# w2's seven products: the sums R1, R6 and R7 over the chunks in DRAM, by adding transfers, instead of in SBUF by the vector engine

## The chip, the core and the metric

One core of one Trainium2 chip runs the whole program. The time is that of the device, in microseconds (us), from one launch; several runs give a median. Beside it there is one profiled execution, whose trace gives the start and the length of every instruction.

Five engines work at the same time, each through its own list of instructions in order: TensorE (PE in the profile; its weight loads are PEld), VectorE (DVE), ScalarE (ACT), GpSimd (POOL) and SyncE (SP). An instruction that waits holds up everything behind it on its engine. SP issues the loads of the weights; in the part that matters here POOL has little else to do than to issue transfers too.

## What is computed

One layer of a network over 384 tokens (128 of a context, 256 latent ones) with D_MODEL 2048, all in float32. The change lies in the second half of the MLP:

```python
h = _rmsnorm(x, norm_w[2]) * (1 + scale_f) + shift_f
y = jnp.square(jax.nn.relu(h @ w1)) @ w2          # w1: 2048 x 8192, w2: 8192 x 2048
x = x + gate_f * _rmsnorm(y, norm_w[3])
```

## The kernel before, in words

**Precision.** Each matrix product is made of three matmuls: both operands are split in a rounded part hi and a remainder lo, and hi·hi, hi·lo and lo·hi are summed in PSUM. So each tile of weights (128 x 1024) is loaded by SP into a raw buffer, copied to hi by ACT (L134, L1189), and subtracted into lo by DVE (L135, L1190) before PE can use it.

**The MLP.** The 8192 rows of w2 are worked through in eight chunks `ch` of 1024 (`for ch in range(8)`). In a chunk the kernel makes that part of the hidden layer (`w1_group`, four groups of 256 hidden channels) and multiplies it by the chunk's rows of w2, in four blocks `n` of 512 output columns. The groups of w1 for the next chunk stand between the blocks of w2. The result is summed over the chunks in SBUF, in `y[0]` (context tokens), `y[1]` and `y[2]` (the two halves of the latent tokens).

**The seven products.** Chunk 0 multiplies in the ordinary way (`mlp_out`). Chunks 1 to 6 use `mlp_seven` for all four blocks, chunk 7 for blocks 0 and 1: 26 blocks in all. There the latent tokens are multiplied by a fast scheme: tokens, rows of w2 and columns are each halved, and seven products of quarters, R1 to R7, take the place of eight. DVE makes the sums and differences of w2's quarters (L1225, L1231, L1235, L1239). The products stand in halves of PSUM banks of 512 columns: bank "16" holds R1 and R6, bank "23" R2 and R3, "45" R4 and R5, and the right half of "x7" holds R7 (its left half, and bank "yz", belong to the context tokens). R2 to R5 belong to one output quarter each, and `add` puts them into `y` at once. R1, R6 and R7 belong to several quarters, so they are summed over the chunks by themselves: `r16` (128 x 512 for each block `n`) and `r7` (128 x 256). In the first such chunk, 1, ACT copies the banks into them (L1246, L1247); in the 22 later blocks DVE adds the banks onto them (`add`, L1212).

**The end of the sums.** `seven_done(n)` (L1250 on) combines the finished sums into `y[1]` and `y[2]` by six DVE instructions (L1258 to L1264). For blocks 2 and 3 that is after chunk 6; for blocks 0 and 1 it stands in `done_late`, which chunk 7's last part calls step by step (`mlp_out` with `done`). Then `done` squares `y` on ACT (L1128) and multiplies it by the gate on DVE (L1133), `norm_y` makes the norm, and `residual` adds the input and stores the result (L1144, L1145).

**What sets the order.** The program's text is not the order of the instructions: a scheduler places each engine's list, apart from the last block of all (`last_part`, whose DVE instructions stand as written). SBUF tiles come from pools with a fixed number of buffers: four for hi and lo, three for one half of the raw tiles and two for the other, and 55 `slot` tiles. Chunk 7 begins with `load_tail`, which has POOL load the gate (`gf`) and the residual's input (`x1t`) into slots, each as a slot comes free. So POOL waits there for matmuls that read the slots last.

Of the kernel before, what the change touches and what calls it, by code (L numbers as in the profile page):

```python
# [7 lines left out]
F32 = mybir.dt.float32  # L8
F32R = mybir.dt.float32r
AF = mybir.ActivationFunctionType  # L10
ALU = mybir.AluOpType
AX = mybir.AxisListType

P = 128
# [29 lines left out]
def hymba_kernel(  # L44
# [6 lines left out]
    nc = tc.nc  # L51
# [8 lines left out]
    dram = ctx.enter_context(tc.tile_pool(name="dram", bufs=1, space=bass.MemoryType.DRAM))  # L60
# [401 lines left out]
    for s in range(NS):  # L462
        for ci, (kind, c0, w) in enumerate(chunks):
            k0, nk = ksteps[s]
            hi, lo, n = w_first if s == 0 and ci < 2 else load_chunk(s, ci, h_ins if s == 0 else ())
# [704 lines left out]
        for _ in side:  # L1170
            pass

    def mlp_seven(ch, n, strp, r16, r7, feeds=()):


        k0, c0, first = 8 * ch, 512 * n, ch == S_FIRST
# [16 lines left out]
        def product(m, half, row, tok, w, start=True, stop=True, js=range(4)):  # L1193

            acc = banks[m][:, 256 * half:256 * half + 256]
            for j in js:
                t = k0 + 2 * j
                xh, xl = hid["s", t + 1] if row == 2 else hid[t + row]
                xh, xl = xh[:, tok * P:(tok + 1) * P], xl[:, tok * P:(tok + 1) * P]
                if m == "x7" and half and ch > S_LAST:  # L1200
                    xh, xl = hid["d", t + 1]
                wh, wl = (v[:, 256 * j:256 * j + 256] for v in w)
                nc.tensor.matmul(acc, xh, wh, start=start and j == 0, stop=False)  # L1203
                nc.tensor.matmul(acc, xh, wl, start=False, stop=False)  # L1204
                nc.tensor.matmul(acc, xl, wh, start=False, stop=stop and j == 3)  # L1205
            if tok:
                for f in feeds:
                    f()

        def add(dst, m, half=None):  # L1210
            src = banks[m] if half is None else banks[m][:, 256 * half:256 * half + 256]
            nc.vector.tensor_tensor(dst, src, dst, op=ALU.add)  # L1212
# [29 lines left out]
        add(ys[0], "yz")  # L1242
        w = split(b21, "t4")
        product("45", 0, 1, 2, w)
        if first:
            nc.scalar.activation(r7[:, n], banks["x7"][:, 256:], AF.Copy)  # L1246
            nc.scalar.activation(r16[:, n], banks["16"], AF.Copy)  # L1247
        else:
            add(r7[:, n], "x7", 1)
            add(r16[:, n], "16")  # L1250
        add(ys[2], "45")

    def seven_done(n, r16, r7):

        tt = nc.vector.tensor_tensor
        ys = [y[i][:, 512 * n:512 * n + 512] for i in range(3)]
        r1, r6, v = r16[:, n, 0:256], r16[:, n, 256:], r7[:, n]
        tt(ys[1][:, 0:256], ys[1][:, 0:256], r1, op=ALU.add)  # L1258
        tt(r6, r6, r1, op=ALU.add)
        tt(v, v, r6, op=ALU.add)  # L1260
        tt(r6, r6, ys[2][:, 256:], op=ALU.add)
        tt(ys[1][:, 256:], ys[1][:, 256:], r6, op=ALU.add)
        y2 = ys[2].rearrange("p (a q) -> p a q", a=2)
        tt(y2, y2, v.unsqueeze(1).to_broadcast([P, 2, 256]), op=ALU.add)  # L1264
# [4 lines left out]
    for ch in range(8):  # L1269
        if ch < S_FIRST:  # L1270
            w1_group(4, (ff, fx), 386)
            mlp_out(ch, (ff, fx, fn))
            fn.finish()
            for g in range(5, 8):
                w1_group(g, (ff,))
        elif ch <= S_LAST:
            if ch == S_FIRST:
                fx.finish()
                while not vec.get("half"):
                    next(ff.gen)  # L1280
                for scope in (xb_scope, acc_scope, ada_scope):
                    scope.close()
                str_scope = ExitStack()
                strp = str_scope.enter_context(tc.tile_pool(name="strp", bufs=1, side="right", reuse_waits="tile"))
                vec.update(pool=strp, acc=strp, slab=512, bufs=3, half=False)
                ff.rate = RATE_GS
                r16, r7 = strp.tile([P, 4, 512], F32, name="r16"), strp.tile([P, 4, 256], F32, name="r7")
            for n in range(4):
                mlp_seven(ch, n, strp, r16, r7, (ff,))
                if n == 1:  # L1290
                    w1_group(4 * ch + 4, (ff,))
            if ch == S_LAST:
                ff.finish()
                for n in range(N_LAST, 4):
                    seven_done(n, r16, r7)
            for g in range(1, 4):
                w1_group(4 * ch + 4 + g, (ff,))
        else:
            load_tail()
            for n in range(N_LAST):  # L1300
                mlp_seven(ch, n, strp, r16, r7)

            def done_late():
                for n in range(N_LAST):
                    seven_done(n, r16, r7)
                    yield
                    for i in range(3):
                        done(i, 512 * n, 512 * n + 512)
                        yield

            fd = Feed(done_late(), 1.0)
            ws = mlp_out(ch, (fd,), done, N_LAST)
            fd.finish()
# [56 lines left out]
```

## Time and profile before

| | |
|---|---|
| median of 3 runs | 1690.77 us (1688.34 to 1690.98) |
| span of the profiled execution | 1686.4 us, 27861 instructions |
| PE busy | 1657.3 us (98%) |
| DVE busy | 1341.7 us (80%) |
| ACT busy | 752.3 us (45%) |
| POOL busy | 130.9 us (8%) |
| the last of the 26 blocks of seven products | ends on PE at about 1643.1 us of the span |

The profile gives the profiled execution's span, from its first to its last instruction, and no other time for it. The median run is 4.4 us longer than this span, the shortest run 1.9 us: what lies around the span (the start and the end of the program) is not in the trace.

How to read it: a row of the timeline gives the start, the length, the engine, the line, and how many instructions it stands for, and in brackets how long the engine sat idle before it and what ended that. The chain is followed back from the last instruction, at each step to what released it. Rows of a window give the time in which each engine was busy in that stretch. Matmuls are pipelined, and each is shown longer than its distance to the next.

### The profile page before, as it was taken

The page shows a single profiled execution, that of the slowest core. Times are in us where ns is not written, and L with a number is a line of the kernel's source. Part 1 is how long each engine was busy: PE and PEld are TensorE (multiplying, and loading weights), DVE is VectorE, ACT ScalarE, POOL GpSimd, SP SyncE. Part 2 cuts the span into 40 slices and gives each one's busy share as a digit, 9 for nine tenths or more (in the row PEclk, how much of TensorE's full clock was granted, in tenths as well). Part 3 has the DMA queues.
Part 4 walks back from the last instruction along what each step waited for, and adds up shares of the span by engine and source line. Part 5 has one row for each costly group of instructions (what it writes and reads, how often), then busy time and mean ns, then how long its engine had stood idle before and what let it go on. Part 6 is the DMA issues. An engine that isn't in the chain of part 4 may idle for free.

```text
span 1686.4 us, 27861 instructions
## 1 busy us (share of the span) xinstructions
PE 1657.3 (98%) x10965; PEld 1583.9 (94%) x10965; DVE 1341.7 (80%) x2009; ACT 752.3 (45%) x1225; POOL 130.9 (8%) x181
## 2 busy tenths in 40 slices
PE   6999999999999999999999999999999999999997
PEld 3888999999999989988999999999999999999996
DVE  3677769898998959997797688988588588588688
ACT  4432355555443345543444444444444444444443
POOL 0000002221000023530000000000000000000120
PEclk9999999999999999999999999999999999999999
DMA  9999858776789964754556245544344443443653
GB/s 305 324 297 304 276 153 256 245 248 221 236 265 308 312 206 126 218 153 137 157 169 195 87 138 178 155 150 142 109 150 127 124 139 113 149 125 111 185 184 134
DMA packets 258195, 320.95 MB, mean 190 GB/s; under 512 B 14752, under 2 KB 223248, under 8 KB 257680
## 3 DMA queue, kind: packets, MB, share of 16 engines
q1 hardware_dynamic: 250256, 303.41, 57.1%
q0 software_dynamic: 5856, 13.69, 2.8%
q10 hardware_dynamic: 1952, 2.07, 0.4%
q8 instruction: 86, 1.41, 0.3%
q14 instruction: 45, 0.37, 0.1%
HBM read 308.61 MB, written 10.51 MB: 189 GB/s over the span
## 4 chain that ended last, share of the span: by engine, by line
PE 83%; DVE 9%; DMA 3%; issue 2%; SPq 1%; ACT 1%; POOL 0%; DVEq 0%; ACTq 0%; POOLq 0%
PE acc_w L144 9%; PE acc_w L143 9%; PE acc_w L145 9%; PE v L476 4%; PE y L1204 4%; PE y L1203 4%; PE y L1205 4%; PE u L476 4%; PE acc_wo L143 3%; PE acc_wo L144 3%; PE acc_wo L145 3%; PE y_yz L1203 2%; PE y_yz L1205 2%; PE y_yz L1204 2%; DVE ada_acc L316 2%
## 5 line engine op out<-in xcount | busy, mean ns | idle before, releaser
L144 PE MATMUL acc_w<-h2l,hi_w 128*128 128x384 f32 (+1 forms) x1024 | 346.2, 338 | 0.5 <-DVE h2l L997 0.5
L143 PE MATMUL acc_w<-h2h,hi_w 128*128 128x384 f32 (+1 forms) x1024 | 344.2, 338 | 1.4 <-ACT h2h L993 1.2
L145 PE MATMUL acc_w<-h2h,lo_w 128*128 128x384 f32 (+1 forms) x1024 | 345.1, 337 | 0.0
L135 DVE TENSOR_TENSOR lo_w<-raw_w,hi_w 128x1024 fp32r<-128x1024 f32 x152 | 185.5, 1222 | 134.2 <-ACT hi_w L134 133.7
L134 ACT ACTIVATE hi_w<-raw_w 128x1024 fp32r<-128x1024 f32 x152 | 160.7, 1058 | 211.8 <-PE acc_w L144 95.2
L316 DVE SCALAR_TENSOR_TENSOR ada_acc<-ada_raw,sg,ada_acc 128x1024 f32<-128x1024 f32 (+1 forms) x240 | 252.1, 1082 | 1.9 <-DMA ada_raw<-in_ada_w_dram 1.9
L143 PEld LDWEIGHTS acc_w<-h2h,hi_w 128*128 128x128 f32 x1024 | 192.2, 188 | 3.1 <-ACT h2h L993 2.0
L144 PEld LDWEIGHTS acc_w<-h2l,hi_w 128*128 128x128 f32 x1024 | 192.5, 188 | 1.2 <-DVE h2l L997 0.8
L145 PEld LDWEIGHTS acc_w<-h2h,lo_w 128*128 128x128 f32 x1024 | 192.4, 188 | 0.3 <-DVE lo_w L135 0.2
L1189 ACT ACTIVATE hi_t<-w 128x1024 fp32r<-128x1024 f32 x104 | 109.6, 1060 | 118.6 <-DVE w L1225 33.6
L1190 DVE TENSOR_TENSOR lo_t<-w,hi_t 128x1024 fp32r<-128x1024 f32 x104 | 126.4, 1221 | 15.1 <-ACT hi_t L1189 14.7
L1190 DVE TENSOR_TENSOR lo_b<-w,hi_b 128x1024 fp32r<-128x1024 f32 x78 | 95.3, 1222 | 40.5 <-ACT hi_b L1189 40.4
L1189 ACT ACTIVATE hi_b<-w 128x1024 fp32r<-128x1024 f32 x78 | 82.6, 1060 | 99.2 <-PE acc_w L144 65.9
L134 ACT ACTIVATE hi_wo<-raw_wo 128x1024 fp32r<-128x1024 f32 x32 | 34.0, 1064 | 83.5 <-DMA raw_wo<-in_w_out_dram 65.7
L923 ACT ACTIVATE z<-acc_w 128x384 f32<-128x384 f32 x54 | 26.3, 487 | 75.0 <-PE acc_w L145 75.0
L476 PE MATMUL v<-hi_v,hh 128*128 128x384 f32 (+1 forms) x144 | 47.8, 332 | 0.0
L476 PE MATMUL v<-lo_v,hh 128*128 128x384 f32 (+1 forms) x144 | 46.6, 324 | 0.0
L476 PE MATMUL v<-hi_v,hl 128*128 128x384 f32 (+1 forms) x144 | 46.5, 323 | 0.0
L134 ACT ACTIVATE hi_v<-raw_v 128x768 fp32r<-128x768 f32 (+1 forms) x24 | 18.9, 795 | 60.8 <-DMA raw_v<-in_w_in_dram 40.9
L135 DVE TENSOR_TENSOR lo_wo<-raw_wo,hi_wo 128x1024 fp32r<-128x1024 f32 x32 | 38.8, 1216 | 8.3 <-ACT hi_wo L134 7.5
L143 PE MATMUL acc_k<-hh,hi_k 128*128 128x384 f32 x128 | 44.2, 345 | 0.0
L143 PE MATMUL acc_o<-hh,hi_o 128*128 128x384 f32 x128 | 43.9, 343 | 0.0
(2264 smaller groups left out, 4552.8 us busy)
## 6 DMA issues: line engine op xcount, KB each, us to landing
raw_w<-in_w_dram SPq DMA_DIRECT2D x152, 512.0 KB, 4.3
ada_raw<-in_ada_w_dram SPq DMA_DIRECT2D x130, 512.0 KB, 5.1
w<-in_w_dram SPq DMA_DIRECT2D x104, 512.0 KB, 4.2
raw_wo<-in_w_out_dram SPq DMA_DIRECT2D x32, 512.0 KB, 5.2
u<-in_ada_w_dram SPq DMA_DIRECT2D x18, 512.0 KB, 6.1
raw_u<-in_w_in_dram SPq DMA_DIRECT2D x16, 512.0 KB, 7.1
raw_q<-in_w_in_dram SPq DMA_DIRECT2D x16, 512.0 KB, 4.6
raw_k<-in_w_in_dram SPq DMA_DIRECT2D x16, 512.0 KB, 4.9
```

The costliest lines, as they stand in the source:

```text
L134: nc.scalar.activation(hi[:, 0:n], raw[:, 0:n], AF.Copy)
L135: low = lambda: nc.vector.tensor_tensor(lo[:, 0:n], raw[:, 0:n], hi[:, 0:n].bitcast(F32), op=ALU.subtract)
L143: nc.tensor.matmul(ps, lh, rh, start=start, stop=False)
L144: nc.tensor.matmul(ps, lh, rl, start=False, stop=False)
L145: mm3.ins = nc.tensor.matmul(ps, ll, rh, start=False, stop=stop).ins
L316: nc.vector.scalar_tensor_tensor(acc[:, g, :], raw[:, a, :], cj, acc[:, g, :], op0=ALU.mult, op1=ALU.add)
L476: nc.tensor.matmul(acc[i][:, 0:n], h[k0 + k][a][:, i * P:(i + 1) * P], (hi, lo)[b][:, k, :], start=k == 0 and a + b == 0, stop=k == nk - 1 ...
L1189: nc.scalar.activation(hi, raw, AF.Copy)
L1190: nc.vector.tensor_tensor(lo, raw, hi.bitcast(F32), op=ALU.subtract)
L1203: nc.tensor.matmul(acc, xh, wh, start=start and j == 0, stop=False)
L1204: nc.tensor.matmul(acc, xh, wl, start=False, stop=False)
L1205: nc.tensor.matmul(acc, xl, wh, start=False, stop=stop and j == 3)
```

## The change

`r16` and `r7` go away. Instead there are four tiles in DRAM, `r_dram[n]` of 128 x 768, and a staging tile of two buffers in SBUF. In every block ACT copies R7 and then R1 with R6 from PSUM to the staging tile. In chunk 1 POOL issues a plain transfer of it to DRAM; in the 22 later blocks POOL issues a transfer that adds the tile onto what stands in DRAM. `seven_done` first loads the sums back into a staging tile, also issued by POOL, and then does the same six additions.

```diff
     def mlp_seven(...)
...
+        st = strp.tile([P, 768], F32, tag="stage", name=f"stage_{ch}_{n}", bufs=2)
+        nc.scalar.activation(st[:, 512:], banks["x7"][:, 256:], AF.Copy)
+        nc.scalar.activation(st[:, 0:512], banks["16"], AF.Copy)
         if first:
-            nc.scalar.activation(r7[:, n], banks["x7"][:, 256:], AF.Copy)
-            nc.scalar.activation(r16[:, n], banks["16"], AF.Copy)
+            nc.gpsimd.dma_start(r_dram[n], st)
         else:
-            add(r7[:, n], "x7", 1)
-            add(r16[:, n], "16")
+            nc.gpsimd.dma_start(r_dram[n], st, accum_op=ALU.add)
         add(ys[2], "45")
...
-    def seven_done(n, r16, r7):
+    def seven_done(n, r_dram):
...
-        r1, r6, v = r16[:, n, 0:256], r16[:, n, 256:], r7[:, n]
+        st = strp.tile([P, 768], F32, tag="stage", name=f"sums_{n}", bufs=2)
+        nc.gpsimd.dma_start(st, r_dram[n])
+        r1, r6, v = st[:, 0:256], st[:, 256:512], st[:, 512:]
...
-                r16, r7 = strp.tile([P, 4, 512], F32, name="r16"), strp.tile([P, 4, 256], F32, name="r7")
+                r_dram = [dram.tile([P, 768], F32, name=f"r_dram{n}") for n in range(4)]
```

PE's list of instructions is the same before and after. DVE's is 44 shorter, ACT's 44 longer and POOL's 30 longer (26 transfers to DRAM and 4 back). The scheduler also shifts some of DVE's other work, in places by a few instructions.

Three places matter below. The names are the program's tiles with their buffer numbers, which differ between the two programs.

First, DVE at the start of block 1 of chunk 3, which follows on block 0. `r_8460` is `r7`, `r_8459` is `r16`; `y_0_x`, `y_0_16` and `y_0_45` are block 0's banks, `lo_1_b` and `w_3_1` belong to block 1's weights. Before:

```order
L1190 TENSOR_TENSOR lo_1_b_11380<-w_3_1_00_11366,hi_1_b_11379 128x1024
L1212 TENSOR_TENSOR r_8460<-y_0_x_11183,r_8460 128x256
L1190 TENSOR_TENSOR lo_1_b_11384<-w_3_1_10_11368,hi_1_b_11383 128x1024
L1212 TENSOR_TENSOR r_8459<-y_0_16_11185,r_8459 128x512
L1212 TENSOR_TENSOR y_4990<-y_0_45_11187,y_4990 128x512
L1225 TENSOR_TENSOR w_3_1_00_11366<-w_3_1_01_11372,w_3_1_00_11366 128x1024
L1227 TENSOR_TENSOR y_4988<-y_1_x_11374,y_4988 128x512
L1190 TENSOR_TENSOR lo_1_b_11442<-w_3_1_11_11370,hi_1_b_11441 128x1024
```

After:

```order
L1190 TENSOR_TENSOR lo_1_b_11400<-w_3_1_00_11386,hi_1_b_11399 128x1024
L1225 TENSOR_TENSOR w_3_1_00_11386<-w_3_1_01_11392,w_3_1_00_11386 128x1024
L1190 TENSOR_TENSOR lo_1_b_11404<-w_3_1_10_11388,hi_1_b_11403 128x1024
L1212 TENSOR_TENSOR y_4990<-y_0_45_11205,y_4990 128x512
L1190 TENSOR_TENSOR lo_1_b_11462<-w_3_1_11_11390,hi_1_b_11461 128x1024
L1227 TENSOR_TENSOR y_4988<-y_1_x_11394,y_4988 128x512
```

The two adds onto `r` (128 x 256 and 128 x 512) are gone, and the difference of w2's quarters (L1225) moves up by three places.

Second, POOL near the end, in chunk 7. `x1t` are the loads of the residual's input, `stage_0` and `stage_1` the staged products of blocks 0 and 1, `sums` the finished sums on their way back, and `ry` the exponent of the norm. Before:

```order
L1119 DMA x1t_384_16578<-x_dram 128x384
L1119 DMA x1t_768_16580<-x_dram 128x384
L1119 DMA x1t_1152_16582<-x_dram 128x384
L1119 DMA x1t_1536_16584<-x_dram 128x384
L1119 DMA x1t_1920_16586<-x_dram 128x128
L200 TENSOR_TENSOR ry<-ry,mhalf 128x1 x3
```

After:

```order
L1119 DMA x1t_1152_16636<-x_dram 128x384
L1251 DMA r_dram_8459<-stage_0_16822 128x768
L1119 DMA x1t_1536_16638<-x_dram 128x384
L1119 DMA x1t_1920_16640<-x_dram 128x128
L1259 DMA sums_17039<-r_dram_8459 128x768
L1251 DMA r_dram_8460<-stage_1_17007 128x768
L1259 DMA sums_17152<-r_dram_8460 128x768
L200 TENSOR_TENSOR ry<-ry,mhalf 128x1 x3
```

The load of block 0's sums stands behind the last two loads of `x1t`, and the last transfer of block 1 and the load of its sums behind that.

Third, DVE in the last but one stretch of chunk 7, where block 1's sums are combined. `lo_w_56_3` to `lo_w_60_3` are weights of the last block. Before (`r_8459` and `r_8460` are here block 1's sums, L1258 on are `seven_done`):

```order
L135 TENSOR_TENSOR lo_w_56_3_17089<-raw_w_56_3_17086,hi_w_56_3_17088 128x1024
L1258 TENSOR_TENSOR y_4989<-y_4989,r_8459 128x256
L1259 TENSOR_TENSOR r_8459<-r_8459 128x256
L135 TENSOR_TENSOR lo_w_58_3_17101<-raw_w_58_3_17098,hi_w_58_3_17100 128x1024
L1260 TENSOR_TENSOR r_8460<-r_8460,r_8459 128x256
L1261 TENSOR_TENSOR r_8459<-r_8459,y_4990 128x256
L1262 TENSOR_TENSOR y_4989<-y_4989,r_8459 128x256
L1264 TENSOR_TENSOR y_4990<-y_4990,r_8460 128x512
L135 TENSOR_TENSOR lo_w_60_3_17111<-raw_w_60_3_17108,hi_w_60_3_17110 128x1024
L1069 TENSOR_TENSOR y_4988<-y_2_0_16954,y_4988 128x512
```

After (L1261 on are the same additions; the two rows ahead of them are the gate for block 0, and `lo_w_56_3` stands before those):

```order
L1133 TENSOR_TENSOR y_4990<-y_4990,gf_0_16584 128x384
L1133 TENSOR_TENSOR y_4990<-y_4990,gf_384_16588 128x128
L1261 TENSOR_TENSOR y_4989<-y_4989,sums_17152 128x256
L1262 TENSOR_TENSOR sums_17152<-sums_17152 128x256
L1263 TENSOR_TENSOR sums_17152<-sums_17152 128x256
L1264 TENSOR_TENSOR sums_17152<-sums_17152,y_4990 128x256
L135 TENSOR_TENSOR lo_w_58_3_17163<-raw_w_58_3_17160,hi_w_58_3_17162 128x1024
L1265 TENSOR_TENSOR y_4989<-y_4989,sums_17152 128x256
L1267 TENSOR_TENSOR y_4990<-y_4990,sums_17152 128x512
L135 TENSOR_TENSOR lo_w_60_3_17173<-raw_w_60_3_17170,hi_w_60_3_17172 128x1024
L1069 TENSOR_TENSOR y_4988<-y_2_0_17012,y_4988 128x512
```

The additions now read the loaded tile `sums`; `lo_w_58_3` has moved behind four of the six.

More of the change, by code (lines that the diff above doesn't have):

```diff
@@ L1171, in last_part, with mlp_seven @@
             pass
-    def mlp_seven(ch, n, strp, r16, r7, feeds=()):
+    def mlp_seven(ch, n, strp, r_dram, feeds=()):
         k0, c0, first = 8 * ch, 512 * n, ch == S_FIRST
@@ L1286, in hymba_kernel @@
                 ff.rate = RATE_GS
-                r16, r7 = strp.tile([P, 4, 512], F32, name="r16"), strp.tile([P, 4, 256], F32, name="r7")
+                r_dram = [dram.tile([P, 768], F32, name=f"r_dram{n}") for n in range(4)]
             for n in range(4):
-                mlp_seven(ch, n, strp, r16, r7, (ff,))
+                mlp_seven(ch, n, strp, r_dram, (ff,))
                 if n == 1:
@@ L1294, in hymba_kernel @@
                 for n in range(N_LAST, 4):
-                    seven_done(n, r16, r7)
+                    seven_done(n, r_dram)
             for g in range(1, 4):
@@ L1300, in hymba_kernel @@
             for n in range(N_LAST):
-                mlp_seven(ch, n, strp, r16, r7)
+                mlp_seven(ch, n, strp, r_dram)
             def done_late():
                 for n in range(N_LAST):
-                    seven_done(n, r16, r7)
+                    seven_done(n, r_dram)
                     yield
```

## The prediction

> **What bounds the kernel now.** I read the page first: who is busy, and which engine the chain that ended last runs on.
>
> ```profile
> span 1686.4 us, 27861 instructions
> PE 1657.3 (98%) x10965; PEld 1583.9 (94%) x10965; DVE 1341.7 (80%) x2009; ACT 752.3 (45%) x1225; POOL 130.9 (8%) x181
> PE 83%; DVE 9%; DMA 3%; issue 2%; SPq 1%; ACT 1%; POOL 0%; DVEq 0%; ACTq 0%; POOLq 0%
> ```
>
> PE is the bound over the whole span, but that is an average. The change touches only the part from 832 us on, so the second view is PE's waits in 832 to 1686.4 us, which has a single row, and the third is the busy time in four stretches: chunk 1, a plain stretch of chunk 6, the blocks of chunk 7, and the end.
>
> ```profile
> PE y_yz L1204 <- DVE lo_b L1190: 0.4, 1, 0.4
> core 0: us, PE busy (x) PEld busy (x) DVE busy (x) ACT busy (x) POOL busy (x), PEclk, DMA share, GB/s
> 832.50:911.00 78.50, 77.98 (x610) 77.38 (x609) 75.99 (x93) 39.61 (x49) 0.00 (x0) 1.00 0.54 164
> 1490.00:1560.00 70.00, 70.00 (x547) 70.00 (x547) 60.38 (x71) 32.87 (x36) 0.00 (x0) 1.00 0.45 135
> 1620.00:1660.00 40.00, 40.00 (x271) 36.77 (x270) 36.75 (x51) 18.17 (x22) 1.61 (x3) 1.00 0.44 144
> 1660.00:1686.40 26.40, 16.88 (x97) 14.52 (x95) 19.73 (x50) 7.14 (x21) 1.97 (x3) 0.90 0.34 120
> ```
>
> In the stretch of chunk 6 PE is busy for all of 70.00 us while DVE has 60.38 us of work: DVE is loaded, yet nobody waits for it. In chunk 1 DVE is at 75.99 of 78.50 us, and there PE does wait, once, for 0.4 us. The fourth view is the chain in order of time, which leaves out the shortest pieces, such as single matmuls. Between the second and the third row here it has no row of any engine.
>
> ```profile
> 904.89 1.13 DVE w L1239
> 906.62 1.14 DVE lo_t L1190
> 1658.70 0.69 DVE y L1069
> 1662.59 3.13 DVE y L1133 x10
> 1665.86 0.69 DVE y L1157
> 1680.59 2.38 DVE y L1144 x5
> ```
>
> The last matmul, and DVE's use of it, from the timeline:
>
> ```profile
> 1676.60 0.28 PE L1047 MATMUL y<-hi_w,hid63l 128*128 128x256 f32 x1
> 1676.94 0.42 DVE L1157 TENSOR_TENSOR y<-y,y 128x256 f32<-128x256 f32 x1
> ```
>
> So the kernel has three regimes: chunk 1, where DVE is nearly the bound (up to 907 us); PE alone from there to 1658.70 us; and from 1658.70 us on DVE, step by step, with the last matmul at 1676.60 us and 1686.4 - 1676.9 = 9.5 us of serial end behind it.
>
> **The adds that go.** The rows of the tile `r`, from the view by tile:
>
> ```profile
> L1212 DVE TENSOR_TENSOR r<-y_x,r x22: 414/418/427, 975.3 to 1640.9; 128x256 f32<-128x256 f32 x22
> L1212 DVE TENSOR_TENSOR r<-y,r x22: 681/684/694, 976.8 to 1642.4; 128x512 f32<-128x512 f32 x22
> L1246 ACT ACTIVATE r<-y_x x4: 363/385/386, 843.5 to 908.1; 128x256 f32<-128x256 f32 x4
> L1247 ACT ACTIVATE r<-y x4: 598/598/600, 844.9 to 909.4; 128x512 f32<-128x512 f32 x4
> L1258 DVE TENSOR_TENSOR y<-y,r x4: 412/418/419, 1558.8 to 1652.0; 128x256 f32<-128x256 f32 x4
> L1264 DVE TENSOR_TENSOR y<-y,r x4: 681/684/685, 1563.5 to 1655.2; 128x512 f32<-128x512 f32 x4
> ```
>
> DVE loses 22 x (0.418 + 0.684) = 24.2 us. All of it lies between 975.3 and 1643.1 us, in the regime where PE waits for no one. What hides it today is PE's own work, so its removal is worth **0**: the next thing that is late is still PE. Only the pairs of chunk 7's blocks come near the last regime. They could let DVE reach 1658.70 us with less queued, but its row there waits for PE (below), and DVE met the end of the last matmul (1676.88 us) at 1676.94 us already: at most 0.1 us, and I take 0.
>
> **The copies that come.** ACT gains 22 x (0.385 + 0.598) = 21.6 us in a regime where it is half idle (32.87 of 70.00 us). A copy that waits for a product holds up the next weights' hi behind it. Chunk 1 has the same order already, with four copies of each kind, and the view by line gives all waits of L1246 as one row:
>
> ```profile
>   PE y_x L1205: 1.0, 3
> ```
>
> That is 1.0 us in three times, on an engine with slack, and in that stretch, the tightest of all, PE waited 0.4 us. I take 0; if that cover were gone, each copy could cost PE its length.
>
> **The transfers.** 26 to DRAM and 4 back, of 128 x 768 x 4 bytes = 384 KB. No row shows an adding transfer. The nearest are POOL's plain ones, from the issues (KB each, median us to landing), with the weights' loads beside them, and the page's row of GB/s in 40 slices, whose highest value is 324:
>
> ```profile
> w<-in_w_dram SPq DMA_DIRECT2D x104, 512.0 KB, 4.2
> x_dram<-x1b POOLq DMA_DIRECT2D x64, 48.0 KB, 3.6
> x1t<-x_dram POOLq DMA_DIRECT2D x15, 192.0 KB, 4.1
> GB/s 305 324 297 304 276 153 256 245 248 221 236 265 308 312 206 126 218 153 137 157 169 195 87 138 178 155 150 142 109 150 127 124 139 113 149 125 111 185 184 134
> ```
>
> A plain 384 KB lands in an estimated 4.1 to 4.2 us, between x1t and w. An adding one has to bring the old value too: between 4.1 us, if that costs nothing, and 3 x 4.1 = 12.3 us, if reading the tile, reading DRAM and writing DRAM follow one another like three transfers. I take 6, nearer to the low end, since a transfer of 48 KB takes 3.6 us already and the size therefore is not what its time consists of. While chunks run, nobody waits for these: the next transfer onto the same `r_dram[n]` is a whole chunk away. Nor do they fill the DMA engines: their share is 0.45 in chunk 6, and 393,216 bytes at 324 GB/s are 1.2 us, once in (1640.9 - 975.3) / 21 = 32 us.
>
> **Chunk 1** is where a load is on the path. In block 2, at 892.80 us ACT makes the second copy; DVE then waits for a load of w, and PE waits for DVE:
>
> ```profile
> 892.80 0.60 ACT L1247 ACTIVATE r<-y 128x512 f32<-128x512 f32 x1
> 896.79 1.22 DVE L1225 TENSOR_TENSOR w<-w,w 128x1024 f32<-128x1024 f32 x1 [0.99 <-DMA w<-in_w_dram]
> 900.40 0.39 PE L1204 MATMUL y_yz<-lo_b,hid9h 128*128 128x256 f32 x1 [0.40 <-DVE lo_b L1190]
> ```
>
> The new plain transfer is issued at 893.4 us, beside that load. It can delay it by 0 to 1.2 us, which PE then loses for good, because it never idles again before 1658.70 us. I take **+0.6**.
>
> **The end** is where a transfer is on the path. After block 1 of chunk 7 the chain is: ACT's copy of the bank "16", the adding transfer, POOL's wait for it, the load, six additions on DVE, and behind these in DVE's list `lo_w_58_3` and `lo_w_60_3`. POOL's and PE's rows, and DVE's rows of before:
>
> ```profile
> 1639.94 1.11 POOL L1119 DMA_DIRECT2D x1t<-x_dram  x2 [12.49 <-PE y_x L1205]
> 1640.57 1.06 ACT L134 ACTIVATE hi_w<-raw_w 128x1024 fp32r<-128x1024 f32 x1 [0.34 <-ACT hi_w L134]
> 1641.60 0.28 PE L1205 MATMUL y<-hi_t,hs63l 128*128 128x256 f32 x1
> 1643.34 0.69 DVE L1212 TENSOR_TENSOR y<-y,y 128x512 f32<-128x512 f32 x1
> 1646.29 1.22 DVE L135 TENSOR_TENSOR lo_w<-raw_w,hi_w 128x1024 fp32r<-128x1024 f32 x1
> 1651.98 0.41 DVE L1258 TENSOR_TENSOR y<-y,r 128x256 f32<-128x256 f32 x1
> 1657.00 1.23 DVE L135 TENSOR_TENSOR lo_w<-raw_w,hi_w 128x1024 fp32r<-128x1024 f32 x1 [1.07 <-ACT hi_w L134]
> 1658.70 2.09 DVE L1069 TENSOR_TENSOR y<-y,y 128x512 f32<-128x512 f32 x3 [0.47 <-PE y L1047]
> ```
>
> Block 0's sums first. Their load stands on POOL behind the two x1t, which wait for PE until 1639.94 us; it is issued at 1641.05 us and lands at about 1645.2. DVE wants it at some 1644 us (1643.34 + 0.69). It stalls for 1.2 us, and `lo_w_60_2` (1646.29 before) comes no later than before, since two adds, 1.1 us, are gone ahead of it. Cost 0.
>
> Block 1's sums: "16" is complete at 1641.88 us and ACT is free of `hi_w` at about 1642.0 (the first copy, 0.385, now stands ahead of that `hi_w`); the second copy ends at 1642.6. The adding transfer lands 6 us later, at 1648.6, POOL issues the load, and it lands at 1652.8. DVE wants it at 1652.0. From there to the row at 1658.70 DVE has five additions of 0.42, one of 0.68 and two lo of 1.22, that is 5.2 us; so a start by 1658.70 - 5.2 = 1653.5 us costs nothing. The chain has 1653.5 - 1642.6 = 10.9 us for both transfers and by my estimate takes 10.2. I take **0**, with 0 to +5.6 as bounds: 12.3 us for the adding transfer gives 1642.6 + 12.3 + 4.2 = 1659.1, less 1653.5 us.
>
> The Trainium skill has a price for this in "DMA: Bandwidth & Descriptors", section "Anatomy of one DMA — SWDGE (gpsimd) path": about 2.0 us plus the bytes over 436 GB/s, that is 2.9 us for each of the two. By that estimate the sums would land at 1648.4 us, and the end would cost 0 with 5 us to spare. The trace does not agree: x1t, half that size, took 4.1 us, so the sum goes by 4.1.
>
> **The sum:** 1686.4 + 0 (adds) + 0 (copies) + 0.6 (chunk 1) + 0 (end) = 1687.0 us of span. The median run is 1690.77 - 1686.4 = 4.4 us longer than the profiled span, which the change does not touch: **1691.4 us**. A measurement of this kernel can tell about 0.2% (3.4 us) from no change.
>
> **Rivals.**
> *The adding transfer is slow, and the end waits for it.* Place: block 1's sums in chunk 7. It decides from the point at which both transfers take more than 10.9 us; then everything on DVE from 1658.70 us on, which is the chain, moves by the excess. For it: my estimate leaves 0.7 us of room, and no row shows such a transfer. Against it: plain ones land in 3.6 to 4.2 us. With 12.3 us it gives 1691.4 + 5.6 = 1697.0 us, slower. On top of chunk 1's 0.6 us it needs 2.8 us to pass 3.4, so the adding transfer has to take over 10.9 + 2.8 - 4.2 = 9.5 us. The Trainium skill, in "DMA: Bandwidth & Descriptors", section "Rules for kernel authors", says that such a transfer reads its destination and writes it later, and that an access to the same bytes has to wait for its semaphore; no run here shows how long that is.
> *ACT becomes the head of the weights.* Its copies wait for products, with hi copies behind them. If all 21.6 us came out on PE: 1691.4 + 21.6 = 1713.0. Against it: chunk 1's order is that order.
> *The freed DVE makes it faster.* All 24.2 us would give 1691.4 - 24.2 = 1667.2; the row of PE's waits, 0.4 us in 854 us, speaks against any of it: 1690.3 if that wait and the 0.1 us at the end went too.
> That the change does not do what it says I leave out: the lists show the adds gone and the transfers there.
>
> **How the numbers follow.** Forecast (nothing but chunk 1's 0 to 1.2 us and up to 2 us at the end): 0.80. Slow transfer: 0.12 over 3.4 us. ACT: 0.03. Faster by over 3.4 us: 0.05, mostly since the median of three runs moves between 1688.34 and 1690.98. That gives 0.05, 0.80 and 0.15. The range reaches from 1688.3 (no cost, and a run 2.4 us under its median, as the shortest of before) to 1697.0 (the bound of the slow transfer).
>
> **What would show it.** PE's waits from 911 to 1658 us stay at nothing, while DVE's busy time falls by some 24 us and ACT's rises by some 22. The adding transfer's row of issues gives its landing: up to about 6 us, and the end holds. A wait of DVE's L1261 for `sums` at 1652 us or later, with L1069 moved past 1658.7, would show the slow transfer; waits of PE for hi from 911 us on would show ACT. A span shorter by more than 1 us would make the whole reading wrong.

## The result, and the profile after

| | before | after |
|---|---|---|
| median of the runs, us | 1690.8 (1688.34 to 1690.98) | 1697.24 (1695.2 to 1699.66) |
| the profiled run's own time, us | 1688.34 (by its span, see below) | 1699.66 |
| its span, us | 1686.4 | 1697.9 |
| ratio of the runs, with its 95% interval | | 1.0042 (1.003 to 1.0054) |

The changed kernel is slower, by some 7 us. The forecast was "no change", 1691.4 us, and the measured time lies just above the top of the range, 1697.0. One run of those below, of e6, took 3309.3 us; the ratios leave it out.

The two profiles exaggerate the difference. In the profile of after, 1.8 us lie around the span (1699.66 - 1697.9). If it is about the same before, the profile of before belongs to the shortest run, 1688.34 us, while that of after belongs to the longest. So the comparison goes by stretches. The ends of the stretches are read from the trace: PE's first matmul of chunk 1, its first of chunk 2, the end of block 1 of chunk 7 (the last matmul that reads `hs63l`), the next start of DVE's L1069, and the end of the span.

```
                              before    after   difference
start to chunk 1              830.4     833.8      +3.4
chunk 1                       131.0     134.6      +3.5
chunk 2 to block 1 of ch. 7   680.4     683.5      +3.0
from there to L1069            16.8      18.6      +1.8
L1069 to the end               27.7      27.5      -0.2
```

The first row belongs to no edit: up to chunk 1 the change touches nothing, and that stretch was between 828.9 and 833.8 us long in the fourteen profiles of this study. The other three are what has to be explained. The page of after, its first row, the busy times and the shares of the chain that ended last:

```profile
span 1697.9 us, 27940 instructions
PE 1662.0 (98%) x10965; PEld 1586.1 (93%) x10965; DVE 1319.1 (78%) x1965; ACT 769.2 (45%) x1269; POOL 154.2 (9%) x211
PE 83%; DVE 8%; DMA 5%; issue 2%; ACT 1%; POOL 0%; DVEq 0%; SPq 0%; ACTq 0%; POOLq 0%
```

DVE lost 22.6 us and ACT gained 16.9, where the prediction's parts said 24.2 and 21.6, and PE is at 98% as before. In the chain the share of DMA went from 3% to 5%. PE's waits in the last 866 us, one row of 0.4 us before, are now:

```profile
PE y_yz L1204 <- DVE lo_b L1190: 3.0, 3, 1.3
PE y L1204 <- DVE lo_t L1190: 1.8, 1, 1.8
```

PE waits for DVE's lo again. The 1.8 us (`lo_t`, at 898.4 us) and 1.2 us of the 3.0 (`lo_b`, at 907.3 us) lie in chunk 1. The same view for 911 to 1660 us, which had no row at all before, has one:

```profile
PE y_yz L1204 <- DVE lo_b L1190: 1.9, 2, 1.3
```

Both of these waits are in chunk 3, in blocks 1 and 3 (at 1118.6 and 1168.2 us). Why DVE, with less to do, is late there, shows in its own list. The start of block 1 of chunk 3 on DVE, before:

```profile
1105.03 1.23 DVE L1190 TENSOR_TENSOR lo_b<-w,hi_b 128x1024 fp32r<-128x1024 f32 x1 [1.01 <-ACT hi_b L1189]
1106.17 0.42 DVE L1212 TENSOR_TENSOR r<-y_x,r 128x256 f32<-128x256 f32 x1
1106.51 1.22 DVE L1190 TENSOR_TENSOR lo_b<-w,hi_b 128x1024 fp32r<-128x1024 f32 x1
1107.64 0.69 DVE L1212 TENSOR_TENSOR r<-y,r 128x512 f32<-128x512 f32 x1
1108.24 0.69 DVE L1212 TENSOR_TENSOR y<-y,y 128x512 f32<-128x512 f32 x1
1109.59 1.23 DVE L1225 TENSOR_TENSOR w<-w,w 128x1024 f32<-128x1024 f32 x1 [0.67 <-DMA w<-in_w_dram]
```

and after:

```profile
1111.97 1.23 DVE L1190 TENSOR_TENSOR lo_b<-w,hi_b 128x1024 fp32r<-128x1024 f32 x1 [1.01 <-ACT hi_b L1189]
1116.19 1.23 DVE L1225 TENSOR_TENSOR w<-w,w 128x1024 f32<-128x1024 f32 x1 [3.00 <-DMA w<-in_w_dram]
1117.34 1.22 DVE L1190 TENSOR_TENSOR lo_b<-w,hi_b 128x1024 fp32r<-128x1024 f32 x1
```

The second of the two lo, that of b21, started 1.5 us after the first before (1106.51 - 1105.03) and 5.4 us after it now. The difference L1225 stands between them, and it needs b12, the last of the block's four loads. DVE stands still for 3.00 us with the lo of b21 behind it, whose hi was ready at 1113.6 us by ACT's row:

```profile
1112.57 1.05 ACT L1189 ACTIVATE hi_b<-w 128x1024 fp32r<-128x1024 f32 x1
```

The chain of after at that place (start, length, what) shows what the load waits for, and who waits at the end:

```profile
1109.14 1.24 DVE lo_t L1190
1110.39 5.71 DMA w<-in_w_dram
1116.43 0.91 issue
1117.34 1.23 DVE lo_b L1190
1118.61 0.40 PE y_yz L1204
```

The load is issued in the moment in which block 0's last `lo_t` is done, 1110.38 us. `raw2` has two buffers, and block 0's b21 and b12 hold them; the load needs the one that comes free last. (The trace has no buffer numbers, so which of the two that is does not show.) The load lands 5.7 us later, and then DVE's difference, DVE's lo and PE follow on one another.

The load itself is no later than it was. Before, it was issued at 1103.45 us, 1.6 us ahead of the lo of b11 as after, and it ended DVE's wait at 1109.59 us, 6.1 us later, with no new transfer in the program. What differs is what DVE has to do before it needs the load.

L1225 waits in blocks 1 and 3 of chunks 2 to 6 and in block 1 of chunk 7, 0.9 to 3.7 us each, and nowhere else but once in chunk 1. All waits of L1225 in the trace, first before, then after:

```profile
  DMA w<-in_w_dram: 1.7, 2
```

```profile
  DMA w<-in_w_dram: 23.9, 12
```

Most of the 23.9 us DVE can afford: PE waits for 1.9 us of it, and the stretch is 3.0 us longer.

At the end, the chain of after:

```profile
1652.81 7.87 DMA r_dram<-stage
1660.68 0.28 issue
1660.96 4.69 DMA sums<-r_dram
1665.68 0.43 DVE y L1261
...
1669.43 1.14 DVE lo_w L135
1670.56 1.49 DVE y L1069 x3
```

The two transfers are on the path: 7.87 and 4.69 us. Block 1's products end at 1651.87 us, the sums are back at 1665.65, 13.8 us later, and L1069 no longer waits for PE (0.47 us before) but follows directly on the lo that stands behind the sums.

DVE's own rows there show that the transfers were not the only thing that was late:

```profile
1655.62 0.42 DVE L1261 TENSOR_TENSOR y<-y,sums 128x256 f32<-128x256 f32 x1 [1.46 <-DMA sums<-r_dram]
1659.46 1.22 DVE L135 TENSOR_TENSOR lo_w<-raw_w,hi_w 128x1024 fp32r<-128x1024 f32 x1 [1.61 <-ACT hi_w L134]
1663.74 1.43 DVE L1133 TENSOR_TENSOR y<-y,gf 128x384 f32<-128x384 f32 x4
1665.68 0.43 DVE L1261 TENSOR_TENSOR y<-y,sums 128x256 f32<-128x256 f32 x1 [0.51 <-DMA sums<-r_dram]
```

The first L1261 is block 0's, the last is block 1's. Block 1's waits only 0.51 us for its sums: 1.46 us that DVE waited for block 0's sums and 1.61 us for a hi had made DVE late already. With block 1's sums in time, L1069 would have come only some 0.5 of the 1.8 us earlier.

### The profile page after: what moved, and what is told of

Read it like the earlier page. It is cut to its first block, busy times and chain, and to the rows that moved or that the text cites. A ratio compares the mean times of both kernels' runs of the same rounds, so it can differ in the third digit from the quotient of the medians.

```text
span 1697.9 us, 27940 instructions
## 1 busy us (share of the span) xinstructions
PE 1662.0 (98%) x10965; PEld 1586.1 (93%) x10965; DVE 1319.1 (78%) x1965; ACT 769.2 (45%) x1269; POOL 154.2 (9%) x211
## 4 chain that ended last, share of the span: by engine, by line
PE 83%; DVE 8%; DMA 5%; issue 2%; ACT 1%; POOL 0%; DVEq 0%; SPq 0%; ACTq 0%; POOLq 0%
PE acc_w L143 9%; PE acc_w L144 9%; PE acc_w L145 9%; PE y L1204 4%; PE y L1205 3%; PE y L1203 3%; PE v L476 3%; PE u L476 3%; PE acc_wo L143 3%; PE acc_wo L144 3%; PE acc_wo L145 3%; PE y_yz L1204 2%; PE y_yz L1203 2%; PE y_yz L1205 2%; PE acc_o L143 1%
## 5 line engine op out<-in xcount | busy, mean ns | idle before, releaser
L1251 POOL DMA_DIRECT2D r_dram<-stage x22 | 18.8, 855 | 623.1 <-ACT stage L1247 591.6
L1225 DVE TENSOR_TENSOR w<-w,w 128x1024 f32<-128x1024 f32 x26 | 31.9, 1225 | 24.4 <-DMA w<-in_w_dram 23.9
```

## The experiments

Each kernel was timed beside the kernel before on the same chip. Two theories stand against each other. **A**: the costs are the moved difference, which waits for a load, and the sums' way back at the end (in e1 to e3 it also counts chunk 1's stores). **B**: the new transfers cost, beside the weights' loads. One table for all, with the ratio to before and its interval, and the stretches of each profile in us:

```
                            ratio   95% interval      to ch.1  ch.1   ch.2-7   to L1069
before                                                 830.4   131.0  680.4    16.8
the change                  1.0042  1.003  to 1.0054   833.8   134.6  683.5    18.6
the change again (e11)      1.0048  1.0032 to 1.0063   833.7   135.5  682.9    19.6
e1  old order               1.0021  1.0012 to 1.003    830.7   135.1  680.1    19.2
e2  new order alone         1.0053  1.0042 to 1.0065   829.0   132.8  690.8    16.8
e3  four stores alone       1.0005  0.9997 to 1.0014   828.9   134.7  680.4    16.8
e4  early sums              1.0023  1.0014 to 1.0032   829.4   135.1  682.5    16.8
e5  old order, early sums   1.0003  0.9994 to 1.0012   831.5   136.2  681.0    16.8
e6  no adds, old order      0.9991  0.9982 to 1.0      829.4   132.9  680.4    16.8
e7  plain transfers         1.0037  1.0025 to 1.005    831.9   133.5  682.4    19.4
e8  no transfers in 2 to 6  1.0038  1.0025 to 1.005    833.8   134.2  681.4    19.5
e9  third buffer            1.0006  0.9998 to 1.0015   830.8   131.3  680.4    18.3
e10 third buffer, early s.  0.9987  0.9978 to 0.9995   830.8   132.0  680.4    16.8
e12 no adds, new order      1.0003  0.9993 to 1.0013   830.1   133.0  683.2    16.8
```

**e1, the old order.** The changed kernel, with the difference held behind the lo of b21 in blocks 1 and 3 from chunk 2 on:

```
+        lo_b21 = split.ins          # the lo of b21
...
-        tt(b11, b12, b11, op=ALU.subtract)
+        with tc.issue_after(lo_b21) if n % 2 and not first else ExitStack():
+            tt(b11, b12, b11, op=ALU.subtract)
```

> The change, but in blocks 1 and 3 of chunks 2 to 6 and in block 1 of chunk 7 the first difference of w2's quarters (L1225) is held behind the lo of b21 in DVE's list, as it stood before. Theory A, three causes that add up: the stores of chunk 1 delay loads (about 3.7 us in the profile after), DVE's moved difference waits for a load with a needed lo behind it (2.9 us in chunks 3 and 4), the end waits for the last sums (1.7 us). By A the median falls from 1697.2 to about 1694.3, and PE's waits for lo in chunks 3 and 4 go away. Rival B, the adding transfers slow the loads of w everywhere and the order does not matter: 1697.2, and the waits stay.

Measured: 1694.19 us, ratio 1.0021. The stretch from chunk 2 is back at 680.1 us, and `lo_b` is gone from PE's waits. The order is worth about half of the cost.

**e2, the new order alone.** The kernel before, all in SBUF, with the lo of b21 (made in `split`, the first two lines) held behind the difference in the same blocks:

```
+            with tc.issue_after(behind()) if behind else ExitStack():
+                nc.vector.tensor_tensor(lo, raw, hi.bitcast(F32), op=ALU.subtract)
...
+        swap = n % 2 and not first
+        diff = lambda: tt(b11, b12, b11, op=ALU.subtract).ins
+        wa, wb = split(b11, "b11"), split(b21, "b21", diff if swap else None)
...
+        if not swap:
+            diff()
```

> The kernel before, with nothing but the moved order: in blocks 1 and 3 of chunks 2 to 6 and block 1 of chunk 7 the lo of b21 stands behind the difference L1225 on DVE. The adds stay, no transfer is added. By A 1690.8 + 2.9 = 1693.7 or a little more, since the adds still lie there, with PE waiting for lo of b21 in some blocks after 911 us. By B, 1690.8: without the adding transfers the load is there in time.

Measured: 1698.59 us, ratio 1.0053. No transfer was added, and it costs 9 us, as much as the whole change or more. The sign is A's, the size is not: the stretch from chunk 2 took 690.8 us, 10.4 more than before, where the changed kernel took 3.0 more. e12 below answers that.

**e3, chunk 1's stores alone.** The kernel before, with four plain 384 KB stores of what ACT copied in chunk 1, which nobody reads. `rs` holds `r16` and `r7` side by side, so that one transfer takes both:

```
             nc.scalar.activation(r16[:, n], banks["16"], AF.Copy)
+            nc.gpsimd.dma_start(spare_dram[n], rs[:, n])
...
+                rs = strp.tile([P, 4, 768], F32, name="rs")
+                r16, r7 = rs[:, :, 0:512], rs[:, :, 512:]
```

> The kernel before, with nothing but four plain transfers of 384 KB from the sums to DRAM in chunk 1, as in the change; nobody reads them. By A 1690.8 + 3.7 = 1694.5, with the loads beside the second store landing over 1.5 us later and PE waiting in 832 to 915 us for some 4 us. By the price of the prediction for these stores, 0 to 1.2 us: 1690.8 to 1692.0. By B, which puts it all on the adding transfers, 1690.8.

Measured: 1690.18 us, ratio 1.0005 (0.9997 to 1.0014), that is +0.8 us with -0.5 to +2.4. A's 1694.5 was wrong: the 3.5 us that the profile of after showed in chunk 1 are not the price of the stores in the time. The profile of e3 shows them all the same, 134.7 us against 131.0, though its run took 1690.18 us; so the one profile of before, of a short run, is no safe base for this stretch.

**e4, the sums loaded early.** The changed kernel, but the sums of blocks 0 and 1 are loaded ahead of chunk 7, and DVE adds its two blocks onto them as before:

```
+        if ch > S_LAST:
+            add(early_sums[n][:, 512:], "x7", 1)
+            add(early_sums[n][:, 0:512], "16")
+        else:
             (staging and transfer as in the change)
...
+            for n in range(N_LAST):
+                early_sums[n] = load_sums(n, "early")
             load_tail()
```

> The change, but the sums of blocks 0 and 1 are loaded back ahead of chunk 7, and chunk 7's own two blocks are added to them on DVE as before: the end has no transfer on its path (and DVE's order in block 1 of chunk 7 is the old one). By A 1697.2 - 1.7 = 1695.5, and DVE no longer waits for sums after 1650 us. If the end's wait is covered after all, 1697.2.

Measured: 1693.56 us, ratio 1.0023. From block 1's end to L1069 it is 16.8 us again, as before. It gave more in time, 3.2 us by the two ratios, than the 1.8 us of the one profile. The other profiles with a transfer there have 18.3 to 19.6 us, so 1.5 to 2.8; and in block 1 of chunk 7 the difference is back in its old place here.

**e5, both repairs.**

> The changed kernel with both repairs: the difference of w2's quarters stands behind lo of b21 again, and the sums of blocks 0 and 1 are loaded before chunk 7, whose two blocks DVE adds as before. All copies and transfers of chunks 1 to 6 are kept. Theory A (two causes, the order and the end, and the transfers beside the chunks cost next to nothing): 1697.2 less the two gains measured apart, 3.0 and 3.6, gives 1690.6 us, the same as the kernel before within 0.2%; PE's waits add up to no more than 4 us. Rival B (26 transfers that triple the DRAM traffic of the sums slow the weights' loads): stays above 1693.5 us, since all of them up to chunk 6 are there.

Measured: 1689.44 us beside 1689.45 of before, ratio 1.0003. As A had it: all copies and all transfers of chunks 1 to 6 are there, and the whole costs less than can be told. It is a net price, since 20 of the 22 pairs of additions are gone too, which e6 below puts at 0 to 3 us. B, with its 1693.5 us, is out. The four kernels add up: 0.5 us (e5), 3.4 for the order (e4 less e5), 3.0 for the end (e1 less e5), together 6.9 against 7.1 and 8.1 (0.42% and 0.48%) in the change's two measurements. By the intervals each of the two differences is good to some 2 us.

**e6, no adds.** The kernel before without the two `add` onto `r`; R1, R6 and R7 of chunks 2 to 7 are left out.

> The kernel before without the 22 pairs of DVE additions onto r, and nothing in their place (left out: R1, R6 and R7 of chunks 2 to 7). DVE's list is otherwise in the same order. Theory A (the prediction's zero: they lie beside PE's work): 1690.1 us, within 1 us of the kernel before. Rival (the additions hold DVE up when a load is late, so their removal is worth something): 1687 us or less. If A holds, the change had nothing to gain, and all that it adds shows.

Measured: 1688.26 us, ratio 0.9991 (0.9982 to 1.0). DVE's busy time on the page:

```profile
span 1687.1 us, 27816 instructions
PE 1657.0 (98%) x10965; PEld 1582.6 (94%) x10965; DVE 1322.3 (78%) x1965; ACT 752.0 (45%) x1225; POOL 130.8 (8%) x181
```

DVE has 19 us less to do, and that is worth between 0 and 3 us: the stretch from chunk 2 stays at 680.4. Its list has the old order. So the missing adds alone did not move the difference. All kernels in which ACT copies and nothing holds the order have the new one, e7 and e8 too.

**e7, plain transfers.** The changed kernel without `accum_op`, so that the sums over the chunks are left out:

```
-            nc.gpsimd.dma_start(r_dram[n], st, accum_op=ALU.add)
+            nc.gpsimd.dma_start(r_dram[n], st)
```

> The changed kernel with plain transfers in place of the adding ones; all else, the moved order too, is kept (left out: the sum over the chunks, only chunk 7's or 6's products remain). Theory A: the transfer at the end lands in about 5 us instead of 7.9, so two transfers take under 10.9 us and the end's 1.7 to 3.6 us go: 1693.6 to 1695.5 us; the order's 3.0 us stay, with DVE's waits for a load at the difference of w2's quarters. Rival B (adding transfers delay the weights' loads in chunks 2 to 6): the waits of the difference shrink to the 2 us of before, and the time falls under 1692 us.

Measured: 1695.9 us, ratio 1.0037. The order's cost stayed, as A had it, but the end's did too (19.4 us to L1069), and there A was wrong. The transfers at the end on POOL, and the page's row of issues:

```profile
1648.62 0.55 POOL L1251 DMA_DIRECT2D r_dram<-stage  x1 [1.45 <-ACT stage L1247]
1655.84 0.54 POOL L1259 DMA_DIRECT2D sums<-r_dram  x1 [6.68 <-DMA r_dram<-stage]
```

```profile
r_dram<-stage POOLq DMA_DIRECT2D x26, 384.0 KB, 5.6
```

The plain one landed in 6.9 us there, and in 5.6 in the median. An adding one took 7.9 to 8.2 us at that place in the five kernels that have one (the change, e1, e8, e9, e11). The same row of after:

```profile
r_dram<-stage POOLq DMA_DIRECT2D x26, 384.0 KB, 5.8
```

In the median no price of the adding can be told: e1 has 5.6 as well, e9 5.7 and e11 6.5. At the end it is about 1 us, but that us was not what L1069 came late by. The load of the sums, issued at 1655.84 us, landed 4.0 us later, at 1659.85. DVE took them up at 1662.25, without a wait:

```profile
1652.45 0.42 DVE L1261 TENSOR_TENSOR y<-y,sums 128x256 f32<-128x256 f32 x1 [2.04 <-DMA sums<-r_dram]
1657.23 1.23 DVE L135 TENSOR_TENSOR lo_w<-raw_w,hi_w 128x1024 fp32r<-128x1024 f32 x1 [2.55 <-ACT hi_w L134]
1660.91 1.43 DVE L1133 TENSOR_TENSOR y<-y,gf 128x384 f32<-128x384 f32 x4
1662.25 0.42 DVE L1261 TENSOR_TENSOR y<-y,sums 128x256 f32<-128x256 f32 x1
```

Here the whole delay is DVE's own, from the wait for block 0's sums and the wait for a hi behind it. So neither the adding nor the way of block 1's sums alone is the price of the end.

**e8, no transfers in chunks 2 to 6.** The changed kernel with the adding transfers of chunk 7 only (the other chunks' share of the sums is left out):

```
-        else:
+        elif ch > S_LAST:
             nc.gpsimd.dma_start(r_dram[n], st, accum_op=ALU.add)
```

> The changed kernel without the adding transfers of chunks 2 to 6 (left out: those chunks' share of R1, R6 and R7); copies, moved order, chunk 1's stores and chunk 7's transfers are kept. Theory A (b12's load is late because its buffer comes free late, and the moved difference waits for it): from chunk 2 to the end of block 1 of chunk 7 it takes 682.5 to 684 us, as the changed kernel's 683.5 and not the 680.4 of before; the difference's idle time at loads stays above 18 us; the time stays at 1695.5 to 1697.5 us. Rival B (the adding transfers slow the weights' loads): idle time under 8 us, that stretch at most 681 us, the time at most 1694.5 us.

Measured: 1696.73 us, ratio 1.0038; L1225 still waits for loads, 20.9 us in 13 times, against 24.6 in 13 in the changed kernel beside it (e11). The time is A's, and B's 1694.5 is out. The stretch from chunk 2, 681.4 us, is 1.1 less than A's lowest value, so that up to 2 us of it may be the transfers'; the two ratios, 1.0038 and 1.0048, can't tell.

**e9, a third buffer.** The changed kernel with `raw2` at three buffers, for which the SBUF that the sums left has room. The order is the new one:

```
-            raws[r, c] = pool.tile([P, 1024], F32, tag=tag, name=f"w2_{ch}_{n}_{r}{c}", bufs=3 - m % 2)
+            raws[r, c] = pool.tile([P, 1024], F32, tag=tag, name=f"w2_{ch}_{n}_{r}{c}", bufs=3)
```

> The changed kernel with a third buffer for the raw tiles of b21 and b12 (raw2), which the SBUF freed from the sums has room for; the moved order is kept. b12's load then need not wait for the block before to be done with its buffer. Theory A (the moved difference costs because it waits for b12's load): its 24 us of idle time at loads fall under 3 us and the time by about the 3.0 us that the old order gave: 1694.2 us, with the end's cost left. Rival (the order costs by the 1.23 us of the difference itself, ahead of a lo that PE is about to need): waits for the load go, but the time stays at 1696.5 us or more.

Measured: 1690.37 us, ratio 1.0006 (0.9998 to 1.0015). The same place of chunk 3 on DVE:

```profile
1105.64 1.23 DVE L1190 TENSOR_TENSOR lo_b<-w,hi_b 128x1024 fp32r<-128x1024 f32 x1 [1.01 <-ACT hi_b L1189]
1106.90 1.23 DVE L1225 TENSOR_TENSOR w<-w,w 128x1024 f32<-128x1024 f32 x1
1108.04 1.22 DVE L1190 TENSOR_TENSOR lo_b<-w,hi_b 128x1024 fp32r<-128x1024 f32 x1
```

The difference stands where it stood in the changed kernel, waits for nothing, and costs nothing: 680.4 us. So the place alone is harmless (the rival of this run is out), and the wait for the buffer is the cause. The gain, 6 us, is more than the 3 expected; chunk 1 went back to 131.3 us as well, and PE's waits in all of the last 856 us are one of 0.6. The end's 18.3 us stay.

**e12, the new order without the adds.** e2 without the two `add`, to see why e2 cost three times what the change pays in that stretch (R1, R6 and R7 of chunks 2 to 7 are left out):

> The kernel before with the new order of the difference alone and without the 22 pairs of additions (left out: R1, R6 and R7 of chunks 2 to 7); no copies, no transfers. With the additions, the new order took 690.8 us from chunk 2 to block 1 of chunk 7. Theory A (the same late load, but a DVE with 1.1 us less to do for each block catches up before PE runs dry): 682.5 to 684.5 us as in the changed kernel, and 1691 to 1693.5 us in all; the additions' removal was worth some 7 us there, not 0. Rival (the order costs what it costs, with or without additions): 688 us or more, 1696 us or more.

Measured: 1691.46 us, ratio 1.0003, and 683.2 us from chunk 2: the changed kernel's 683.5, without one copy or transfer. The time is A's. How the adds make it worse, the same place shows. e2:

```profile
1109.90 1.23 DVE L1221 TENSOR_TENSOR w<-w,w 128x1024 f32<-128x1024 f32 x1 [1.78 <-DMA w<-in_w_dram]
1111.04 0.69 DVE L1213 TENSOR_TENSOR r<-y,r 128x512 f32<-128x512 f32 x1
1111.64 0.68 DVE L1213 TENSOR_TENSOR y<-y,y 128x512 f32<-128x512 f32 x1
1112.24 1.22 DVE L1191 TENSOR_TENSOR lo_b<-w,hi_b 128x1024 fp32r<-128x1024 f32 x1
```

and e12:

```profile
1110.96 1.23 DVE L1221 TENSOR_TENSOR w<-w,w 128x1024 f32<-128x1024 f32 x1 [3.14 <-DMA w<-in_w_dram]
1112.10 1.22 DVE L1191 TENSOR_TENSOR lo_b<-w,hi_b 128x1024 fp32r<-128x1024 f32 x1
```

The wait is longer without the adds, but in e2 two additions queue behind the load and ahead of the lo that PE needs, 1.2 us, and DVE has less slack to make it up in. PE's waits for `lo_b` from 832 us on, in e2 and then in e12:

```profile
PE y_yz L1205 <- DVE lo_b L1191: 6.0, 7, 2.5
```

```profile
PE y_yz L1205 <- DVE lo_b L1191: 2.1, 3, 1.1
```

So the removed adds were worth 0 to 3 us with the old order (e6) and some 8 with the new (1.0053 less 1.0003).

**e10, third buffer and early sums.** e9 and e4 together, the early sums in the staging buffers.

> The changed kernel with the third raw2 buffer and the early loads of the sums of blocks 0 and 1 (chunk 7's two blocks added by DVE as before). Theory A: both costs go, 680.4 us for the middle stretch, 16.8 us from block 1's last product to DVE's first addition of the last stage (18.6 in the changed kernel), and 1689 to 1691 us in all. If it beats the kernel before at all, then by the wait in chunk 1 that the third buffer takes away, at most 1.5 us, within what can be told from no change. Rival (something else in the changed kernel still costs): 1692 us or more.

Measured: 1687.82 us beside 1690.59 of before, ratio 0.9987 (0.9978 to 0.9995): both stretches are at their old lengths, and of the versions that compute everything it is the only one that beats the kernel before, by 2.2 us or 0.13%. That is less than the 0.2% of the prediction, and about what e6 gained by having no sums at all. It stays open whether it comes from the missing adds or from chunk 1's loads.

**e11, the changed kernel again.**

> The changed kernel itself, beside the three others on the same chip, since the shares of its cost are differences from it: 1696 to 1698 us by its four runs so far; the same three stretches within 0.5 us, except chunk 1's, which moves by some 2 us from profile to profile.

Measured: 1699.58 us, ratio 1.0048 (1.0032 to 1.0063), somewhat above the expected times. Middle and end keep their costs; the end's 19.6 us miss the expected half microsecond.

## Why the prediction was wrong, point by point

**The step that failed: the adds that go, and the copies that come, counted at 0 as if the rest of DVE's list stayed.** The description of the change quoted the place, L1225 three places further up, ahead of the lo of b21, and the prediction gave that move no term. It costed what is removed and added, and said of chunks 2 to 7 that PE waits for no one. But L1225 needs the last load of its block, and in its old place it already waited for it by 0.67 us here: two adds, an addition and a lo ahead of it had hidden the rest of that load. The question of what is queued behind a waiting instruction was asked for ACT's copies and for the end, and not for this one. Its cost is 3.4 us (e4 less e5, good to some 2 us) and 3.0 us in the stretch. Four edits show the cause: e1 takes the order away and e9 the wait, and e2 and e12 make the order alone.

**The end, counted at 0 with bounds of 0 to 5.6.** The place was right, it was the main rival, and the stretch showed as described: L1069 later, DVE at L1261 waiting for the sums. It cost 1.8 us in the profile of after, up to 2.8 in others, and 3.0 by e1 less e5. Two steps failed.

The first is the size of block 1's way back. The transfer took 7.9 us instead of 6, the load 4.7 instead of 4.2, and 0.6 us of issue lie between: 13.1 us from the second copy's end for 10.9 us of room, so 2.2 late by the same working. The price was put on the adding, which e7 shows to be about 1 us at this place and none that can be told in the median. What was mis-sized is the plain 384 KB store, 5.6 us in the median and 6.9 here, and not 4.1. The text took the size for a small part of the time (48 KB 3.6 us, 192 KB 4.1 us); the runs don't show why 384 KB from SBUF take 5.6. The estimate of 2.9 us from the Trainium skill, "DMA: Bandwidth & Descriptors", section "Anatomy of one DMA — SWDGE (gpsimd) path", is further off still.

The second is block 0's sums, counted at 0. The stall was about as said, 1.46 us (1.2 said), and the next `lo_w` came 4.42 us after block 1's products, as before (4.41). But the `lo_w` behind it came after 7.59 us and not 6.48, since DVE waited for its hi, which waited for its weights: their load, issued at the same distance as before, took 5.8 us and not 4.2. The two 384 KB transfers and an earlier second load of weights ran beside it; the runs don't show which of them slowed it. DVE was free for block 1's sums only 13.3 us after the products, where the same working needs it after 11.6. So it was 1.7 us late by itself, and the sums made it only 0.5 us more. In e7 and e11 DVE did not wait for block 1's sums at all, in e1 and e8 1.3 us. The runs e4, e5 and e10, which bring the stretch back to 16.8 us, take both ways back away at once, so the shares of the two blocks are a reading of the rows and not measured apart.

That the measured 1697.24 us lies next to the 1697.0 of this rival is chance: the end cost 1.8 to 3.0 of the rival's 5.6 us, and the order, which no rival had, made up most of the rest.

**Chunk 1, +0.6 with 0 to 1.2.** By e3 the stores alone cost +0.8 us (-0.5 to +2.4), so the term stands in time. The profiles say more: 133.5 to 136.2 us in the eight with stores and two buffers, 131.0 to 133.0 in the four without, 131.3 and 132.0 with the third buffer. The medians of the first two groups are 2.0 us apart, above the bound of 1.2. But a profile can be of any run: that of e5, with 136.2, belongs to its longest, 1694.85 us, and the median of e5 is 1689.44, with a possible gain from the missing adds in it. Between 0 and 2.4 us this stays open; 0.6 lies in it.

**ACT's copies and the transfers beside the chunks, 0.** Right as direct costs, as far as can be told: e5 has all but two blocks' share of them and takes as long as before, though the adds that it lacks may hide up to 3 us. But a step that is free on its engine can still go with another order on a second one. In blocks 1 and 3 from chunk 2 on, the difference has moved wherever ACT's copies stand in place of the adds, unless it is held; without adds and without copies (e6) it stays where it was. The copies are not the only thing that can move it: in e10, block 1 of chunk 7 has adds and the new order. By what rule the scheduler places it, the runs don't show.

**"The freed DVE makes it faster", left at 0.05.** Right with the old order (e6: 1.5 us, 0 to 3.0). With the new order the missing adds save some 8 us (e2 against e12), and so they hid most of the order's price.

**The offset of 4.4 us** between the profiled span and the median was taken for something that lies around the span. By the profile of after 1.8 us do; the rest is that this profile was of the shortest run. The sum came out the same.

## What to carry to other kernels

Costing an edit by the instructions it adds and removes is not enough where a scheduler makes the lists: go through every instruction that the new list has moved, ask which of them waits for a load, and what stands ready behind it. A wait for a load can be cured at its source, by a buffer more, and not only by fixing the order: here the SBUF that the change had freed paid for it. And a store and load back near the end of the kernel need their measured time (some 13 us for 384 KB here), and they can make the work beside them late too; here it helped to start the way back a stage earlier and do the last additions in SBUF.

## What the runs showed of the hardware

Adding transfers into DRAM were hardly slower than plain ones of the same shape: 5.6 to 6.5 us in the median of each kernel for 384 KB against 5.6 in e7, and 7.9 to 8.2 against 6.9 at the end. What differs is POOL's time to issue one, by the views of the tile `r_dram`, of after and of e7 (minimum, median and maximum in ns):

```profile
L1251 POOL DMA_DIRECT2D r_dram<-stage x22: 838/850/927, 983.8 to 1652.8; - x22
L1249 POOL DMA_DIRECT2D r_dram<-stage x4: 539/552/587, 849.2 to 917.3; - x4
```

```profile
L1251 POOL DMA_DIRECT2D r_dram<-stage x22: 539/539/558, 980.7 to 1648.6; - x22
```

850 ns adding, 539 to 552 plain: 0.3 us for each, which is nothing while chunks run, on an engine that is 9% busy, and part of the 1 us at the end. A load of 512 KB, 4.2 us in the median, took 5.7 us at the place in chunk 3 where the profile of after has its step, and 6.1 at the same place before.
